# A streaming-encoder block on one core: the second FFN starts with a seven-product pair instead of three token-wise chunks

## The chip, the core and the metric

One NeuronCore of a Trainium2 chip runs the whole kernel. The metric is the device time of one execution in microseconds. The profiler's engine names are kept: PE is TensorE (PEld its weight loads), DVE is VectorE, ACT is ScalarE, POOL is GpSimd, SP is SyncE, whose queue issues most of the DMAs.

## What is computed

A residual block on 256 tokens of width 1024, in float32: a first feed-forward network (FFN), a mixer (a gated linear recurrence beside a causal attention with forgetting, joined by gates), a cross-attention to a memory of 256 rows, and a second FFN. Each part normalises its input, and its output once more ahead of the residual addition. The change touches the second FFN and the stages ahead of it that prepare its weights:

```
h = rmsnorm(x, ffn2_pre_g)
gate, up = split(h @ w_in)          # w_in: 1024 x 5632
x = x + 0.5 * rmsnorm((silu(gate) * up) @ w_down, ffn2_post_g)   # w_down: 2816 x 1024
```

## The kernel before

**Split operands.** TensorE gets every float32 operand as two rounded parts, high and low: ScalarE rounds (`S.copy`), VectorE subtracts (`split`, L155; `load_split` for weights, L129). A product of two operands is three matmuls: high by high, high by low, low by high.

**Tokens and chunks.** The tokens lie in two halves of 128 (`h` 0 and 1), the hidden width in `NFF` = 11 chunks of 256. A *unit* is 128 x 1024 values of a weight, 512 KB. A chunk of `w_in` is four units (gate and up columns of eight blocks of 128 rows, two blocks a unit); a chunk of `w_down` is two. `proj_tok` (L177) multiplies one half of the tokens by one chunk in 24 matmuls of 512 columns; `act_evac` (L414) forms silu(gate) times up, `flush` (L391) and `flush_half` (L405) transpose the result, and `down` (L607) adds its 12 matmuls per half to four accumulators in PSUM.

**Pairs by seven products.** `quad` (L426) takes two chunks and the two token halves as a 2 x 2 by 2 x 2 block product and forms it by a Strassen-Winograd scheme: seven block products of 12 matmuls each instead of eight. It needs four mixed sums of the activations (`mixed`, L289, S1 to S4) and four sums of the weights (T1 to T4). In the second FFN before the change, `QUADS_2` pairs chunks 3-4, 5-6, 7-8 and 9-10. For the first three the weight sums are made earlier: while the mixer and the memory read run, `load_step` (L770) loads weights into one of two `wide` buffers over GpSimd's DMA queue, `at` (L783) makes four additions of 128 x 512 on VectorE at the place that `SUMS_AT` (L56) names, and stores the sums in DRAM, again over GpSimd's queue. There are four steps per pair. `quad` then loads the sums over SyncE's queue (`sum_of`, L446). The last pair makes its sums on the spot.

**The start of the second FFN.** Two chunks are multiplied token-wise, first for half 0, then for half 1 (L617 to L624). Half 1 of the input is not there at the start: the memory read's output projection and its post-norm (`post`, L341, with the reciprocal root `rstd_of`, L220) end with `xs[:, 1]`, and `second` (L1333) transposes it with `to_T` (L319) at the 45th matmul of the FFN (`L_F2` = 44). `to_T` makes four transposes into a PSUM bank and then block by block (`gain_split`, L281) the scaled high part on ScalarE and the low part on VectorE. After the two chunks comes chunk 2, beside which `mixed` rebuilds the whole activation as high plus low (L291 to L294, four blocks of 128 x 256 in each of two additions) and forms S1 to S4; then the first down-projection, and then the pairs.

**What sets the order.** Tile orders the instructions of each engine at compile time, by program order as priority and by a model of when they are ready; it may put a ready instruction of later text ahead of one that is not. `after(n)` pins a group behind the n-th matmul of TensorE, `issue_after` behind a given instruction of the same engine. On the chip each engine then goes strictly in that order.

**Buffers.** Eight pairs of high and low weight buffers of one unit, five `raw` landing buffers, two `wide` ones; in PSUM four banks `acc`, two `mm`, two `tr`.

Of the kernel before, what the change touches and what calls it, by code (L numbers as in the profile page):

```python
# [37 lines left out]
L_F2 = 44  # L38
L_OA = 20
# [14 lines left out]
QUADS_2 = (3, 5, 7, 9)  # L54
# [3 lines left out]
    ("br_a", 1), ("mk", 3), ("mq", 0), ("mq", 1),  # L58
# [20 lines left out]
def block_kernel(ctx: ExitStack, tc: tile.TileContext, wts, head_in, gf_in, x_in, mem_in, memT_in, cols, rows, fbias, masks, out):  # L79
# [209 lines left out]
    def mixed(X, full):  # L289

        if full is None:  # L291
            full = [m4([P, 4, T], n="full") for _ in range(2)]
            for f, xh, xl in zip(full, X.h, X.l):
                V.tensor_tensor(out=f, in0=xh.bitcast(F32), in1=xl.bitcast(F32), op=ALU.add)  # L294
        sums = [m4([P, 2, 4, P], n="sums") for _ in range(2)]
        s1_, s2_, s3_, s4_ = (t[:, i] for t in sums for i in range(2))

        def form(o, x, y, op):
            for q in range(2):
                V.tensor_tensor(out=o[:, 2 * q : 2 * q + 2], in0=x(q), in1=y(q), op=op)  # L300
# [12 lines left out]
        for t in sums:  # L313
            hi, lo = m4([P, 2, 4, P], F32R, "sh"), m4([P, 2, 4, P], F32R, "sl")
            split(hi, lo, t)
            out += [(hi[:, i], lo[:, i]) for i in range(2)]
        return out

    def to_T(X, src, h, g, qs=(0, 1)):  # L319

        for q in qs:
            ps = trp()
            for j in range(4):
                kb = 4 * q + j
                PE.transpose(ps[:, j * P : (j + 1) * P], src(kb), ident)  # L325
# [59 lines left out]
    def ffn(w_in, w_dn, X, full, r2, n_tok, i_row, quads, sums, first_half, second_half=None):  # L385
# [39 lines left out]

        def quad(c, n_down):  # L426
# [6 lines left out]
            def two(src):  # L433
                hi, lo = (p.rearrange("p (i n) -> p i n", i=2) for p in parts_of())
                split(hi, lo, src)
                return [(hi[:, i], lo[:, i]) for i in range(2)]

            B11, B21 = [], []

            if ahead:  # L440
                for i in range(4):
                    hi, lo = load_split(wts[_AT[w_in] + 4 * c + i - 4])
                    B11.append((hi[:, :512], lo[:, :512]))
                    B21.append((hi[:, 512:], lo[:, 512:]))

                def sum_of(k):  # L446
                    W = wp.tile([P, 2, D], F32, tag="wide", name=nm("wide"), bufs=2)
                    for q in range(2):
                        with tc.issue_after(loads[-1]):
                            loads.append(nc.sync.dma_start(W[:, q], sums[c][(0, 3, 2, 1)[k], q]).ins)  # L450
                    return two(W[:, 0].rearrange("p (i n) -> p i n", i=2)) + two(W[:, 1].rearrange("p (i n) -> p i n", i=2))

                def lower():
                    out = []
                    for q in range(2):
                        u = _AT[w_in] + 4 * c + 2 * q
                        raw = wp.tile([P, D], F32, tag="raw", name=nm("raw"), bufs=5).rearrange("p (i n) -> p i n", i=2)
                        loads.append(nc.sync.dma_start(raw, wts[u : u + 2, :, 512:].rearrange("i p n -> p i n")).ins)
                        out += two(raw)
                    return out  # L460

                summed = None
            else:
                wide, made = [], [[], [], []]
# [47 lines left out]

            def block(h, j):
                hs = slice(h * P, h * P + P)
                return lambda i: (X.hi(2 * i + j)[:, hs], X.lo(2 * i + j)[:, hs])

            def F(h, l):
                return lambda i: (h[:, i], l[:, i])

            def prod(ps, A, B, i, start, stop=False):  # L520
                (ah, al), (bh, bl) = A(i), B[i]
                MM(ps, ah, bh, start=start and i == 0, stop=False, skip_group_check=True)
                MM(ps, ah, bl, start=False, stop=False, skip_group_check=True)
                MM(ps, al, bh, start=False, stop=i == 3, skip_group_check=True)

            def prods(ps, A, B, start, stop=False):
                for i in range(4):
                    prod(ps, A, B, i, start, stop)

            def keep(ps):  # L530
                t = sp.tile([P, 512], F32, tag="z2", name=nm("keep"), bufs=3)
                S.copy(t, ps)  # L532
                return t
# [91 lines left out]
        accs = grow = None  # L625
        done = 0
        if callable(r2):
# [6 lines left out]
            n_tok = 2  # L634
        for c in range(n_tok, NFF):
            if c in acts:
                continue
            if c in quads:
                quad(c, done)
                done += 2  # L640
                continue
# [26 lines left out]
            if accs is None:  # L668
                accs = [[acc(), acc()], [acc(), acc()]]
# [80 lines left out]
    def half(X, r, h, g, *ms):  # L750

        for i, m in enumerate(ms):
            with after(m):
                to_T(X, x_blocks(h), h, g, (i,) if len(ms) == 2 else (0, 1))
# [7 lines left out]
    ffn("f1_in", "f1_dn", X1, full1, norm_1, 0, 0, QUADS_1, None, first)  # L762


    sums = {c: dp.tile([4, 2, P, D], F32, name=f"sums_{c}") for c in QUADS_2[:3]}
# [563 lines left out]
    half(X4, r4, 0, G_F2, m + L_MO)  # L1329
# [3 lines left out]
    def second(m):  # L1333
        half(X4, r4, 1, G_F2, m + L_F2)

    ffn("f2_in", "f2_dn", X4, None, r4, 2, 3, QUADS_2, sums, None, second)


# [83 lines left out]
```

## Time and profile before

| | |
|---|---|
| median of 3 runs | 780.89 us (780.45 to 781.83) |
| profiled execution | 780.96 us |
| its span, first to last instruction | 779.2 us |
| granted clock of TensorE | 0.998 |
| TensorE busy | 770.3 us (99%) |
| VectorE busy | 648.4 us (83%) |
| ScalarE busy | 472.4 us (61%) |
| GpSimd busy | 38.7 us (5%) |
| bytes moved by DMA | 182.07 MB, 234 GB/s on average |

A busy time counts the time in which an instruction of the engine is under way; matmuls overlap in the records (each lasts about 0.39 us and the next one issues 0.23 us after it), so TensorE can be 99% busy with some time to spare. The chain that ended last says, from the last instruction backwards, what each step waited for. In the rows of the timeline come start, length, engine, line, operation, output and inputs, and in brackets the idle time of the engine ahead of it with what ended it. A row of busy time by stretches has the stretch, its length, then for each engine busy time and instructions, the granted clock, the share of the DMA engines and GB/s.

### The profile page before, as it was taken

How to read it: one execution, taken by the hardware profiler on the slowest of the kernel's cores; microseconds unless marked ns; L12 is line 12 of the kernel's file. 1: busy time of each engine (PE TensorE's matmuls, PEld its weight loads, DVE VectorE, ACT ScalarE, POOL GpSimd, SP SyncE). 2: the span in 40 equal slices, each digit the busy share in tenths (PEclk: the TensorE clock that was granted, in tenths of full speed). 3: DMA queues.
4: the chain of work that ended last, by engine and by line, in shares of the span. 5: the costliest groups of instructions: out<-in, count | busy, mean ns of one | idle time of the engine just before them, and what ended most of it. 6: DMA issues, size and time to landing. Idle time of an engine off the chain costs nothing.

```text
span 779.2 us, 13049 instructions
## 1 busy us (share of the span) xinstructions
PE 770.3 (99%) x4984; PEld 666.1 (85%) x4984; DVE 648.4 (83%) x995; ACT 472.4 (61%) x711; POOL 38.7 (5%) x64
## 2 busy tenths in 40 slices
PE   9999999999999999999999999999999999999996
PEld 7888878888899999998888888999888888888885
DVE  7799999998886788678787885988767988888994
ACT  7666676577753545447675444744655767777572
POOL 0000000000121000200001220001000000000000
PEclk9999999999999999999999999999999999999999
DMA  9774648378687663754489998468644199779421
GB/s 344 286 264 135 243 143 328 108 231 309 250 289 246 199 211 111 259 189 150 155 309 314 381 337 338 134 223 318 218 154 144 68 341 385 294 283 348 171 81 55
DMA packets 53966, 182.07 MB, mean 234 GB/s; under 512 B 5896, under 2 KB 9360, under 8 KB 53904
## 3 DMA queue, kind: packets, MB, share of 16 engines
q1 hardware_dynamic: 46960, 156.45, 56.6%
q0 software_dynamic: 6800, 24.65, 8.9%
q8 instruction: 39, 0.64, 0.3%
q14 instruction: 23, 0.19, 0.1%
q10 hardware_dynamic: 144, 0.13, 0.0%
HBM read 167.58 MB, written 13.64 MB: 233 GB/s over the span
## 4 chain that ended last, share of the span: by engine, by line
PE 91%; DVE 6%; issue 1%; ACT 1%; DMA 1%; SPq 0%; DVEq 0%; ACTq 0%
PE mm L93 60%; PE acc L93 25%; PE tr L93 3%; DVE lo L157 2%; PE tr L325 1%; PE tr L400 1%; DMA head<-in_head_dram 1%; DVE lo L138 1%; DVE wide L502 1%; ACT hi L156 0%; DVE sum L467 0%; DVE sum L471 0%; DVE sum L489 0%; PE tr L1093 0%; DVE at L421 0%
## 5 line engine op out<-in xcount | busy, mean ns | idle before, releaser
L138 DVE TENSOR_TENSOR lo<-raw,hi 128x1024 fp32r<-128x1024 f32 (+1 forms) x216 | 255.8, 1203 | 49.3 <-ACT hi L137 46.4
L137 ACT CAST hi<-raw 128x1024 fp32r<-128x1024 f32 (+1 forms) x216 | 218.1, 1034 | 94.4 <-PE mm L93 64.5
L93 PE MATMUL mm<-lo,hT 128*128 128x512 f32 (+1 forms) x424 | 161.8, 385 | 0.0
L93 PE MATMUL mm<-hi,hT 128*128 128x512 f32 (+1 forms) x424 | 161.6, 385 | 0.0
L93 PE MATMUL mm<-hi,lT 128*128 128x512 f32 (+1 forms) x424 | 160.5, 383 | 0.0
L93 PE MATMUL acc<-hi,act 128*128 128x512 f32 x352 | 113.2, 390 | 0.0
L93 PE MATMUL mm<-hT,lo 128*128 128x256 f32 x384 | 109.2, 284 | 0.4 <-issue 0.4
L93 PE MATMUL mm<-lT,hi 128*128 128x256 f32 x384 | 109.2, 284 | 0.0
L93 PE MATMUL mm<-hT,hi 128*128 128x256 f32 x384 | 108.9, 283 | 0.0
L93 PEld LDWEIGHTS mm<-hi,hT 128*128 128x128 f32 x424 | 79.6, 188 | 15.3 <-ACT hT L286 0.8
L93 PEld LDWEIGHTS mm<-hi,lT 128*128 128x128 f32 x424 | 79.6, 188 | 15.0 <-DVE lT L287 0.5
L93 PEld LDWEIGHTS mm<-lo,hT 128*128 128x128 f32 x424 | 79.5, 188 | 14.1
L93 PEld LDWEIGHTS acc<-hi,act 128*128 128x128 f32 x352 | 65.9, 188 | 13.5
L93 PEld LDWEIGHTS mm<-hT,lo 128*128 128x128 f32 x384 | 73.6, 192 | 0.6 <-issue 0.6
L93 PEld LDWEIGHTS mm<-lT,hi 128*128 128x128 f32 x384 | 73.6, 192 | 0.2
L93 PEld LDWEIGHTS mm<-hT,hi 128*128 128x128 f32 x384 | 73.6, 192 | 0.1
L93 PE MATMUL acc<-lo,act 128*128 128x512 f32 x176 | 69.1, 393 | 0.0
L156 ACT CAST hi<-wide 128x1024 fp32r<-128x1024 f32 x40 | 41.5, 1054 | 12.8 <-DVE wide L502 9.2
L157 DVE TENSOR_TENSOR lo<-wide,hi 128x1024 fp32r<-128x1024 f32 x40 | 47.7, 1217 | 0.4
L93 PE MATMUL mm<-hi,sh 128*128 128x512 f32 x112 | 43.9, 392 | 0.3 <-ACT keep L532 0.3
L93 PE MATMUL mm<-lo,sh 128*128 128x512 f32 x112 | 43.7, 390 | 0.0
L93 PE MATMUL mm<-hi,sl 128*128 128x512 f32 x112 | 43.6, 389 | 0.0
(249 smaller groups left out, 1146.6 us busy)
## 6 DMA issues: line engine op xcount, KB each, us to landing
raw<-in_wts_dram SPq DMA_DIRECT2D x226, 512.0 KB, 5.1
sums<-wide POOLq DMA_DIRECT2D x24, 512.0 KB, 6.9
wide<-sums SPq DMA_DIRECT2D x24, 512.0 KB, 6.5
wide<-in_wts_dram SPq DMA_DIRECT2D x20, 512.0 KB, 6.6
wide<-in_wts_dram POOLq DMA_DIRECT2D x20, 512.0 KB, 6.7
raw<-in_gf_dram SPq DMA_DIRECT2D x12, 344.0 KB, 5.7
head<-in_head_dram SPq DMA_DIRECT2D x8, 388.0 KB, 6.0
grow<-in_rows_dram SPq DMA_DIRECT2D x4, 512.0 KB, 6.9
```

Of the source, the lines that this page charges most:

```text
L93: log.append(PE.matmul(*args, **kw).ins)
L137: S.copy(h, r)
L138: V.tensor_tensor(out=l, in0=r, in1=h.bitcast(F32), op=ALU.subtract)
L156: S.copy(hi, src)
L157: V.tensor_tensor(out=lo, in0=src, in1=hi.bitcast(F32), op=ALU.subtract)
L325: PE.transpose(ps[:, j * P : (j + 1) * P], src(kb), ident)
L400: PE.transpose(trv[:, j, h * P : (h + 1) * P], ats[c, h][:, j * P : (j + 1) * P], ident)
L502: V.tensor_tensor(out=W[:, :, 0], in0=W[:, :, 0], in1=W[:, :, 1], op=ALU.add)
```

## The change

- The second FFN multiplies only chunk 0 token-wise. `quad_first` takes chunks 1-2 as a pair: its two products of half 0 alone come first, then chunk 0 for half 0, the transposes of half 1 (still at the 45th matmul), chunk 0 for half 1, the product of half 1 alone (T4), the down-projection of chunk 0, and then the four products of mixed sums.
- `QUADS_2` gets chunk 1: five pairs, four of them with sums made ahead. `SUMS_AT` gets four more steps (`br_b` 1, `mk` 1, `mv` 1, `ao` 0), the steps of chunk 1 first in line.
- Of the first pair's four weight sums, T4 and T1 are split into high and low parts on GpSimd (`pool=True`); all other splits stay on ScalarE and VectorE.
- `to_T` can build the whole activation (`full`): four scaled copies on ScalarE into `full`, then one `split` of 128 x 512; for the first four blocks of half 1 it goes block by block as before and adds high and low afterwards. `mixed` no longer rebuilds it.
- The token-wise start for `n_tok` chunks is gone. Helper functions of `quad` move out of it unchanged.

```diff
-QUADS_2 = (3, 5, 7, 9)
+QUADS_2 = (1, 3, 5, 7, 9)
+L_H0 = 4
+L_H1 = 10
 SUMS_AT = (
     ("i_a", 1), ("f_a", 0), ("f_a", 2), ("f_a", 3), ("gates", 1), ("gates", 3), ("br_a", 0), ("br_b", 0),
-    ("br_a", 1), ("mk", 3), ("mq", 0), ("mq", 1),
+    ("br_a", 1), ("br_b", 1), ("mk", 1), ("mk", 3), ("mq", 0), ("mq", 1), ("mv", 1), ("ao", 0),
 )
...
-    def split(hi, lo, src):
-        S.copy(hi, src)
-        V.tensor_tensor(out=lo, in0=src, in1=hi.bitcast(F32), op=ALU.subtract)
+    def split(hi, lo, src, pool=False):
+        (G.tensor_copy if pool else S.copy)(hi, src)
+        (G if pool else V).tensor_tensor(out=lo, in0=src, in1=hi.bitcast(F32), op=ALU.subtract)
...
     def mixed(X, full):
-        if full is None:
-            full = [m4([P, 4, T], n="full") for _ in range(2)]
-            for f, xh, xl in zip(full, X.h, X.l):
-                V.tensor_tensor(out=f, in0=xh.bitcast(F32), in1=xl.bitcast(F32), op=ALU.add)
...
-    def to_T(X, src, h, g, qs=(0, 1)):
+    def to_T(X, src, h, g, qs=(0, 1), full=None):
+        hs = slice(h * P, h * P + P)
         for q in qs:
             ps = trp()
...
+            if full and (h, q) != (1, 0):
+                for j in range(4):
+                    kb = 4 * q + j
+                    S.activation(full[q][:, j, hs], ps[:, j * P : (j + 1) * P], AF.Copy, scale=cols_s[:, g + kb : g + kb + 1])
+                split(X.h[q][:, :, hs], X.l[q][:, :, hs], full[q][:, :, hs])
+                continue
             for j in range(4):
                 gain_split(X, 4 * q + j, ps[:, j * P : (j + 1) * P], g, h * P, h * P + P)
+            if full:
+                V.tensor_tensor(out=full[q][:, :, hs], in0=X.h[q][:, :, hs].bitcast(F32), in1=X.l[q][:, :, hs], op=ALU.add)
...
+        def sum_ahead(c, k, pool=False):
+            W = wp.tile([P, 2, D], F32, tag="wide", name=nm("wide"), bufs=2)
+            for q in range(2):
+                with tc.issue_after(loads[-1]):
+                    loads.append(nc.sync.dma_start(W[:, q], sums[c][(0, 3, 2, 1)[k], q]).ins)
+            return sum((two(W[:, q].rearrange("p (i n) -> p i n", i=2), pool) for q in range(2)), [])
...
+        def quad_first():
+            for k in range(3):
+                acts[k] = m4([P, 2, 2, T], F32R, "act")
+            B11, B21 = left_ahead(1)
+            b1, b3 = mm(), acc()
+            m = len(log)
+            for i in range(4):
+                prod(b1, block(0, 0), B11, i, True)
+                prod(b3, block(0, 1), B21, i, True, True)
+            p1 = keep(b1)
+            V.tensor_tensor(out=p1, in0=p1, in1=b3, op=ALU.add)
+            act_evac(p1, 1, 0)
+            ps = acc()
+            proj_tok(ps, X, chunk(w_in, 0), 0)
+            second_half(m)
+            act_evac(ps, 0, 0)
+            T4 = sum_ahead(1, 3, True)
+            n = len(log)
+            ps = acc()
+            proj_tok(ps, X, chunk(w_in, 0), 1)
+            flush_half(0, 0, n + L_H0)
+            act_evac(ps, 0, 1)
+            late.clear()
+            ready = mixed(X, full)
+            mix.append(ready)
+            (s1h, s1l), (s2h, s2l), (s3h, s3l), (s4h, s4l) = ready
+            T1 = sum_ahead(1, 0, True)
+            n = len(log)
+            b4 = acc()
+            prods(b4, block(1, 1), T4, True, True)
+            u = keep(b4)
+            flush_half(0, 1, n + L_H1)
+            accs[:] = [[acc(), acc()], [acc(), acc()]]
+            for h in range(2):
+                down(0, h)
+            b2 = mm()
+            prods(b2, F(s1h, s1l), T1, True)
+            prods(b1, F(s2h, s2l), sum_ahead(1, 1), False)
+            w = keep(b1)
+            prods(b1, F(s3h, s3l), sum_ahead(1, 2), False, True)
+            v = keep(b1)
+            V.tensor_tensor(out=u, in0=u, in1=v, op=ALU.add)
+            V.tensor_tensor(out=v, in0=b2, in1=v, op=ALU.subtract)
+            act_evac(u, 1, 1)
+            act_evac(v, 2, 1)
+            prods(b2, F(s4h, s4l), lower_ahead(1), False, True)
+            V.tensor_tensor(out=w, in0=b2, in1=w, op=ALU.subtract)
+            act_evac(w, 2, 0)
...
-        for c in range(n_tok):
-            acts[c] = m4([P, 2, 2, T], F32R, "act")
-        for h in range(2):
-            m = len(log)
-            for c in range(n_tok):
-                act_tok(c, h)
-            if h == 0 and n_tok:
-                second_half(m)
...
+        if not first_half:
+            quad_first()
+            done = 1
...
-    sums = {c: dp.tile([4, 2, P, D], F32, name=f"sums_{c}") for c in QUADS_2[:3]}
+    sums = {c: dp.tile([4, 2, P, D], F32, name=f"sums_{c}") for c in QUADS_2[:4]}
...
-    half(X4, r4, 0, G_F2, m + L_MO)
+    full4 = [m4([P, 4, T], n="full") for _ in range(2)]
+    half(X4, r4, 0, G_F2, m + L_MO, full=full4)
...
-    ffn("f2_in", "f2_dn", X4, None, r4, 2, 3, QUADS_2, sums, None, second)
+    ffn("f2_in", "f2_dn", X4, full4, r4, 3, QUADS_2, sums, None, second)
```

More of the change, by code (lines that the diff above doesn't have):

```diff
@@ new lines, in sum_ahead, with lower_ahead @@
+        def sum_ahead(c, k, pool=False):
[4 more added lines that the diff above has]
+            return sum((two(W[:, q].rearrange("p (i n) -> p i n", i=2), pool) for q in range(2)), [])
+        def lower_ahead(c):
+            out = []
+            for q in range(2):
+                u = _AT[w_in] + 4 * c + 2 * q
+                raw = wp.tile([P, D], F32, tag="raw", name=nm("raw"), bufs=5).rearrange("p (i n) -> p i n", i=2)
+                loads.append(nc.sync.dma_start(raw, wts[u : u + 2, :, 512:].rearrange("i p n -> p i n")).ins)
+                out += two(raw)
+            return out
@@ new lines, in prods, with keep @@
+        def prods(ps, A, B, start, stop=False):
+            for i in range(4):
+                prod(ps, A, B, i, start, stop)
+        def keep(ps):
+            t = sp.tile([P, 512], F32, tag="z2", name=nm("keep"), bufs=3)
+            S.copy(t, ps)
+            return t
+        def quad_first():
[4 more added lines that the diff above has]
+            m = len(log)
+            for i in range(4):
+                prod(b1, block(0, 0), B11, i, True)
[39 more added lines that the diff above has]
+            act_evac(w, 2, 0)
@@ L431, in quad @@
                 acts[k] = m4([P, 2, 2, T], F32R, "act")
[L433 to L438, printed above, removed]
             if ahead:
[L441 to L444, printed above, removed]
+                B11, B21 = left_ahead(c)
                 def sum_of(k):
[L447 to L451, printed above, removed]
-                def lower():
[L454 to L460, printed above, removed]
+                    return sum_ahead(c, k)
+                def lower():
+                    return lower_ahead(c)
                 summed = None
             else:
+                B11, B21 = [], []
                 wide, made = [], [[], [], []]
@@ L511, in quad @@
             first = []
[L513 to L533, printed above, removed]
             last = c == NFF - 2
@@ L633, in ffn @@
                     act_evac(outs[c][h], c, h)
-            n_tok = 2
-        for c in range(n_tok, NFF):
+        for c in range(2, NFF):
             if c in acts:
@@ L638, in ffn @@
             if c in quads:
+                if grow is None and sums:
+                    grow = load_row(i_row)
                 quad(c, done)
@@ L667, in ffn @@
                         nc.sync.dma_start(masks_s, masks)
[L668 removed]
+            if not accs:
                 accs = [[acc(), acc()], [acc(), acc()]]
```

35 lines of the change are left out of this document (28 added, 7 removed).

## The prediction

> **What bounds the kernel now.** I read the page first: the span, the busy shares, and the chain that ended last.
>
> ```profile
> span 779.2 us, 13049 instructions
> PE 770.3 (99%) x4984; PEld 666.1 (85%) x4984; DVE 648.4 (83%) x995; ACT 472.4 (61%) x711; POOL 38.7 (5%) x64
> PE 91%; DVE 6%; issue 1%; ACT 1%; DMA 1%; SPq 0%; DVEq 0%; ACTq 0%
> ```
>
> TensorE carries 91% of the chain, so a matmul less counts wherever TensorE is not then kept waiting. Next the chain of waits in order of time, over the start of the second FFN and one later pair.
>
> ```profile
> 597.04 10.44 PE mm L93 x45
> 607.47 0.87 PE tr L325 x8
> 608.35 18.22 PE mm L93 x79
> ...
> 632.03 5.48 PE acc L93 x24
> ...
> 677.08 2.72 PE acc L93 x12
> ```
>
> Twelve 512-column matmuls issue in 2.72 us, 0.2267 us each. From 597.04 to 637.51 only TensorE stands in the chain: matmuls and transposes back to back. So nothing of other engines is waited for at the place that the change rewrites, and whatever it leaves uncovered there is lost at once. Then the table of busy time by stretches: the stage from its first matmul to the first pair, and a steady pair.
>
> ```profile
> core 0: us, PE busy (x) PEld busy (x) DVE busy (x) ACT busy (x) POOL busy (x), PEclk, DMA share, GB/s
> 596.88:637.51 40.63, 40.63 (x186) 32.96 (x185) 37.34 (x77) 26.64 (x46) 0.00 (x0) 1.00 0.51 183
> 674.32:705.25 30.93, 30.93 (x141) 25.48 (x141) 25.63 (x28) 22.62 (x28) 0.00 (x0) 1.00 0.84 318
> ```
>
> The clock is 1.00 throughout. VectorE is busy 37.34 of 40.63 us (92%) at the start and 25.63 of 30.93 us (83%) in a steady pair. GpSimd is idle in both. VectorE is the engine with the least to spare where the work is moved.
>
> **The change part by part.** *The matmuls.* Before, chunks 0, 1 and 2 take 3 x 2 x 24 = 144 matmuls and the first down-projection 24: 168 ahead of the first pair. After, chunk 0 takes 48, the pair 7 x 12 = 84 and the same down-projection 24: 156. Twelve fewer, -2.72 us. That is certain by count; the rest is what stands open.
>
> *The two weight sums on GpSimd.* Each sum is two units of 128x1024, each a one-input copy and a two-input subtraction: eight GpSimd instructions. Their data come early, and their buffers are the ones that the first products release, unit by unit from 596.88 + 6 x 0.2267, about 598.3 us. The last are due at TensorE's 73rd matmul (first sum, about 614 us) and 109th (second, about 623 us), so their own length is covered. Behind them wait the loads of the pair's next two sums, which take over the two `wide` buffers, and in SyncE's queue behind those the weights of chunk 3.
>
> ```profile
> wide<-sums SPq DMA_DIRECT2D x24, 512.0 KB, 6.5
> ```
>
> If GpSimd ends near 613 to 617, these land by 624 (6.5 us); the third product wants the later one near 631. That holds. What GpSimd does to VectorE is not covered. GpSimd's nearest instructions of this size are two selects at 327.53, and I looked at VectorE beside them.
>
> ```profile
> 327.53 3.88 POOL L1053 TENSOR_SCALAR_AFFINE_SELECT cbm<-cbm 128x1024 f32<-128x1024 f32 x2 [6.58 <-DMA cbm<-cd]
> ```
>
> ```profile
> 327.21 1.22 DVE L138 TENSOR_TENSOR lo<-raw,hi 128x1024 fp32r<-128x1024 f32 x1
> ...
> 328.55 1.90 DVE L138 TENSOR_TENSOR lo<-raw,hi 128x1024 fp32r<-128x1024 f32 x1
> 330.38 0.14 DVE L225 TENSOR_SCALAR y<-v 128x1 int32<-128x1 int32 x1
> 330.55 0.86 DVE L227 SCALAR_TENSOR_TENSOR t<-v,y 128x1 f32<-128x1 f32 x1
> 331.45 0.16 DVE L229 SCALAR_TENSOR_TENSOR y<-t,y 128x1 f32<-128x1 f32 x1
> 331.65 0.22 DVE L231 SCALAR_TENSOR_TENSOR t<-v,y 128x1 f32<-128x1 f32 x1
> ```
>
> The split at 328.55 takes 1.90 us where the one before it took 1.22, and a 128x1 operation takes 0.86 where its like takes 0.22; both have two inputs in SBUF. The one-input 128x1 operation at 330.38 stays at 0.14. So I read it as turns: the first select holds VectorE off from 328.43 (327.21 + 1.22) to 329.23 (328.55 + 0.68), 0.80 us, and the second from 330.45 to 331.19, 0.74 us. By the Trainium skill (SBUF — State Buffer, "Who interferes with whom") a VectorE instruction with two SBUF inputs and a GpSimd instruction that reads SBUF shut each other out for a whole instruction. The trace agrees, by 1.90 against 1.22 us.
>
> I take 0.8 us of hold for a copy and twice that, 1.6, for a subtraction, which reads two inputs (an estimate from these rows): 4 x 0.8 + 4 x 1.6 = 9.6 us. The lower bound is 0 if everything falls into VectorE's gaps, the upper 8 x 1.96 (3.88 / 2, waiting included) = 15.7. In exchange VectorE is rid of four splits of 1.2 us, but against the old start it gains as many others (below).
>
> The Trainium skill (GPSIMD Engine Reference, section 3.1) gives 4497 ns for a two-input addition of 2048 elements; half of that, an estimate of 2.25 us each, would add 4 x 0.65 = 2.6 us of hold and, by the share used below, 1.95 us to the sum. No run here shows that operation yet.
>
> Now what VectorE does from 598.85 on, in its timeline and in the table of stretches:
>
> ```profile
> 599.43 0.68 DVE L348 SCALAR_TENSOR_TENSOR post<-acc,grow 128x512 f32<-128x512 f32 x1
> 600.02 0.21 DVE L227 SCALAR_TENSOR_TENSOR t<-v,y 128x1 f32<-128x1 f32 x1
> 600.30 0.61 DVE L287 SCALAR_TENSOR_TENSOR lT<-tr,cols_s,hT 128x128 fp32r<-128x128 f32 x2
> ...
> 601.88 1.21 DVE L138 TENSOR_TENSOR lo<-raw,hi 128x1024 fp32r<-128x1024 f32 x1
> ...
> 604.98 1.42 DVE L352 SCALAR_TENSOR_TENSOR xs<-post,y,xs 128x512 f32<-128x512 f32 x2
> ```
>
> ```profile
> 598.85:606.39 7.54, 7.54 (x34) 6.15 (x33) 7.16 (x26) 4.36 (x10) 0.00 (x0) 1.00 0.56 199
> ```
>
> This is the tail of the memory read's post-norm: two reciprocal-root chains, each with five tiny operations of two inputs (L227 to L235), and then the second half of `xs`, ready at 606.39 us. The transposes of that half start at 607.47, 44 matmuls into the FFN, in TensorE's own order: everything behind them waits with them, and there is no other matmul for half 1. The slack is 1.1 us. The change leaves these chains where they are, saves here five `lT` operations (1.5 us) and adds one of 0.65: without GpSimd `xs` would come at 605.5. About 2.0 us of this stretch (two L348 and the one-input operations) can run beside GpSimd. If the first sum (4.8 us) and half of the second (2.4) get their turns before `xs`, VectorE loses 7.2 - 2.0 = 5.2 us: `xs` at 610.7, TensorE **3.3 us** late at 607.47. Were all eight ahead of it, 9.6 - 2.0 gives 613.1 and 5.6 us; were they all hidden, 0. I take the middle: turns favour GpSimd, since a tiny operation uses one up, but the second sum's buffers come free last.
>
> *The transposed gain of half 0.* Its first four blocks now become four scaled copies, one 128x512 rounding and one subtraction, before any matmul; the old way hands over block by block.
>
> ```profile
> 594.94 0.37 ACT L286 ACTIVATE hT<-tr,cols_s 128x128 fp32r<-128x128 f32 x1
> ...
> 597.85 0.64 ACT L286 ACTIVATE hT<-tr,cols_s 128x128 fp32r<-128x128 f32 x2
> ```
>
> ```profile
> 596.88 0.39 PE L93 MATMUL mm<-hi,hT 128*128 128x512 f32 x1
> ```
>
> Run without a break from 594.94, four copies at 0.3 us, a rounding and a subtraction (0.55 and 0.65 us each as queued) end at 597.3, when the third matmul wants them: 0. With ScalarE's present order, where the fourth block starts at 597.85, they end near 599.3: 2.0 us late. The transposes behind it start that much later too, so this and the wait for `xs` are not added: the larger one, 3.3, stands for both.
>
> *Two copies of a bank with nothing to cover them.* In a steady pair the down-projection runs while ScalarE copies bank `b1`; the new start has used it up, and the third product writes `b1` again at once; the fourth, into `b2`, needs that bank read by VectorE.
>
> ```profile
> 682.13 0.39 PE L93 MATMUL mm<-hi,sl 128*128 128x512 f32 x1
> 682.36 0.39 PE L93 MATMUL acc<-hi,act 128*128 128x512 f32 x1
> ```
>
> ```profile
> 682.55 0.59 ACT L532 COPY keep<-mm 128x512 f32<-128x512 f32 x1 [0.26 <-PE mm L93]
> ...
> 687.99 0.59 ACT L532 COPY keep<-mm 128x512 f32<-128x512 f32 x1 [0.26 <-PE mm L93]
> ```
>
> ```profile
> 688.91 0.68 DVE L565 TENSOR_TENSOR keep<-mm,keep 128x512 f32<-128x512 f32 x1
> ```
>
> There the second product's last matmul issues at 682.13, and the next matmul, of the down-projection, at 682.36. Without it the next would wait for the end of the copy at 683.14: 0.8 us for `w`. For `v` the copy's 0.8 and two VectorE operations of 0.65 follow, 2.1 us; Tile may put the next pair's first products there, so I take half, 1.0. Bounds for the two: 0 (all filled) and 2.9.
>
> *Four more steps of sums in the middle.* Each is four additions on VectorE, four DMAs of 512 KB on GpSimd's queue and no matmul.
>
> ```profile
> 448.93 0.68 DVE L792 TENSOR_TENSOR wide<-wide 128x512 f32<-128x512 f32 x1
> ...
> 451.58 0.68 DVE L795 TENSOR_TENSOR wide<-wide 128x512 f32<-128x512 f32 x1
> ```
>
> ```profile
> 449.00:480.00 31.00, 31.00 (x146) 25.63 (x145) 23.60 (x29) 13.65 (x15) 6.28 (x10) 1.00 0.95 351
> 497.10:519.00 21.90, 21.90 (x185) 21.90 (x185) 20.34 (x50) 16.18 (x32) 0.00 (x0) 1.00 0.47 148
> 560.00:575.00 15.00, 14.91 (x93) 13.03 (x92) 11.12 (x14) 10.70 (x21) 0.00 (x0) 1.00 0.31 106
> 575.00:591.00 16.00, 16.00 (x74) 13.29 (x74) 6.66 (x9) 5.72 (x10) 0.00 (x0) 1.00 0.39 132
> ```
>
> Four at 0.65, about 2.7 us. The steps at `br_b` 1, `mv` 1 and `ao` fall into stretches with 7.4, 3.9 and 9.3 us of VectorE free. `mk` 1 falls into 497 to 519 with 1.6 free: up to 1.1 us, taken as 0.5. The DMA share of 0.95 at 449 could make the `br_b` step wait for its load; the weights behind it have the emptier stretch after 480, so 0.
>
> *The rest* is hidden: `full` built by ScalarE takes two additions off VectorE, the banks turn over as before, and the pairs from chunk 3 on are unchanged.
>
> **The sum.** -2.72 + 3.3 + 0.8 + 1.0 + 0.5 = +2.9 us. The profiled execution took 780.96 us (span 779.2 and 1.8 around it), 0.07 over the median of 780.89; so 780.89 + 2.9 = **783.8 us**.
>
> **The rivals.**
> *Faster.* GpSimd's instructions find VectorE's gaps. For it: 37.34 of 40.63 still leaves 3.3 us, and the saving in `lT` widens it. The place is `xs` of half 1; it decides at 1.1 us of slack plus 0.9 saved, 2.0 us of loss. With that wait at 0, `v` filled by the next pair, and `mk` free: -2.72 + 0.8 = 779.0, at best 778.2. Against it: two-input operations are most of VectorE's list there.
> *About even.* The hold is small but the two copies are paid in full: -2.72 + 2.1 + 0.5, 780.8, reaching from 779.4 to 782.4.
> *Slower elsewhere.* VectorE as a whole becomes the bound. From 596.88 on it needs 37.34 + two more splits (2.4) + four combinations (2.4) - `full` and `lT` (4.0) = 38.1 us in a stage of 40.63 - 2.72 = 37.9, plus about 6.6 of hold that is not beside other work. The lead in splits (six at 1.2, 7.2 us) can swallow 6.8; if half of that is lost, 3.4 us go at the first full pair: -2.72 + 3.4 + 1.8 + 0.5 = 783.9, with 783 to 787 around it, and `xs` on time.
>
> **How the numbers follow.** Forecast (a late `xs`) 0.52, with a range of its own of 782.5 to 789.5 (the upper bound for the hold, 15.7, with some of it covered); faster 0.22; even 0.14; slower elsewhere 0.12. Under 0.2% (1.6 us) a measurement of this kernel can't tell from no change. Faster 0.22, same 0.14, slower 0.64. To leave out no more than 2 in 10 the range must reach into the faster case: 778.4 to 789.5.
>
> **What would show it.** In the new profile: TensorE waiting ahead of the second half's transposes (about 3 us, released by `xs` on VectorE); splits and 128x1 operations on VectorE longer than 1.22 and 0.22 while GpSimd works; waits of 0.8 to 2 us on `keep` at the third and fourth products. The forecast is wrong if VectorE's durations stay as they are beside GpSimd, if `xs` is there at 607.5, or if the next pair's products fill both waits.

## The result: 790.08 us, 1.2% slower, and the profile after

The changed kernel takes 790.08 us (median of 5 runs, 788.7 to 790.57) against 780.45 us (779.81 to 781.83) for the kernel before on the same chip: a ratio of 1.0119, 95% interval 1.0104 to 1.0133. The forecast was 783.8, slower. The direction holds; the time lies 0.6 us above the range.

First the page of the kernel after: span, busy time and the chain that ended last.

```profile
span 788.5 us, 13113 instructions
PE 771.4 (98%) x4972; PEld 666.6 (85%) x4972; DVE 670.3 (85%) x1008; ACT 478.6 (61%) x721; POOL 65.0 (8%) x88
PE 86%; DVE 8%; issue 2%; ACT 1%; DMA 1%; DVEq 0%; ACTq 0%; SPq 0%
```

TensorE's instructions went from 4984 to 4972, the twelve counted; its share of the chain fell from 91% to 86%, and VectorE's rose from 6% to 8%. To find the place, I measure one stage in every kernel: from the last sixteen matmuls of the stage before (`tr` x16 in the chain) to the first row of twelve matmuls of the pair of chunks 5-6 (`mm` x12, the steady pair of the prediction's table). Before:

```profile
573.66 1.92 PE tr L93 x16
...
674.32 2.76 PE mm L93 x12
```

and after:

```profile
574.18 1.92 PE tr L95 x16
...
683.52 2.76 PE mm L95 x12
```

That is 100.66 us before and 109.34 after, 8.7 us of a span that is 9.3 longer. Everything that matters is in this stage. In the timeline of TensorE after, the rows with a wait (in brackets) are these:

```profile
597.77 0.50 PE L95 MATMUL mm<-hi,hT 128*128 128x512 f32 x1 [0.25 <-ACT hT L158]
602.58 0.50 PE L95 MATMUL mm<-hi,lT 128*128 128x512 f32 x1 [0.86 <-DVE lT L159]
609.24 0.50 PE L95 MATMUL acc<-lo,hT 128*128 128x512 f32 x1 [0.25 <-DVE lo L140]
616.72 1.97 PE L324 MATMUL tr<-ident,xs 128*128 128x128 f32 x8 [6.74 <-DVE xs L359]
```

TensorE stands still for 6.74 us ahead of the transposes of half 1, released by `xs` on VectorE: the wait that was forecast, at twice its length. What holds `xs` up stands in the timelines of GpSimd and of VectorE.

```profile
599.58 1.04 POOL L158 CAST hi<-wide 128x1024 fp32r<-128x1024 f32 x1 [15.32 <-PE acc L95]
600.94 1.04 POOL L158 CAST hi<-wide 128x1024 fp32r<-128x1024 f32 x1 [0.32 <-issue]
601.95 6.16 POOL L159 TENSOR_TENSOR lo<-wide,hi 128x1024 fp32r<-128x1024 f32 x2
608.05 3.02 POOL L158 CAST hi<-wide 128x1024 fp32r<-128x1024 f32 x2
611.03 4.63 POOL L159 TENSOR_TENSOR lo<-wide,hi 128x1024 fp32r<-128x1024 f32 x2
```

```profile
599.62 1.01 DVE L237 SCALAR_TENSOR_TENSOR y<-t,y 128x1 f32<-128x1 f32 x1
...
601.33 1.19 DVE L159 TENSOR_TENSOR lT<-full,hT 128x512 fp32r<-128x512 f32 x1
...
602.57 3.29 DVE L140 TENSOR_TENSOR lo<-raw,hi 128x1024 fp32r<-128x1024 f32 x1
605.78 0.14 DVE L227 TENSOR_SCALAR y<-v 128x1 int32<-128x1 int32 x1
605.84 3.35 DVE L140 TENSOR_TENSOR lo<-raw,hi 128x1024 fp32r<-128x1024 f32 x1
609.11 0.99 DVE L229 SCALAR_TENSOR_TENSOR t<-v,y 128x1 f32<-128x1 f32 x1
...
610.62 0.46 DVE L231 SCALAR_TENSOR_TENSOR y<-t,y 128x1 f32<-128x1 f32 x1
611.11 2.27 DVE L233 SCALAR_TENSOR_TENSOR t<-v,y 128x1 f32<-128x1 f32 x1
613.42 2.26 DVE L235 SCALAR_TENSOR_TENSOR t<-t 128x1 f32<-128x1 f32 x1
615.72 0.16 DVE L237 SCALAR_TENSOR_TENSOR y<-t,y 128x1 f32<-128x1 f32 x1
615.91 1.41 DVE L359 SCALAR_TENSOR_TENSOR xs<-post,y,xs 128x512 f32<-128x512 f32 x2
```

The two lists read as turns: all eight GpSimd instructions lie ahead of `xs`, and eight VectorE operations with two inputs are long. Against their usual lengths (0.16 and 0.22 for 128x1, 0.69 for 128x512, 1.2 for a split) they lost 0.85, 0.5, 2.1, 2.15, 0.77, 0.3, 2.05 and 2.1 us, 10.8 together. The two of 128x1 at 611.11 and 613.42 are the plainest: nothing but waiting out one GpSimd subtraction each. The one-input operation at 605.78 keeps its 0.14 us, and an operation of 128x512 with one of its two inputs in PSUM (`keep<-keep,acc` at 610.02) its 0.68.

After the wait TensorE is slow for a while. In the table of stretches the column behind the five engines is the granted clock:

```profile
609.86:616.72 6.86, 0.12 (x2) 0.00 (x1) 6.72 (x8) 0.51 (x1) 5.80 (x4) 0.82 0.64 233
616.72:622.36 5.64, 5.64 (x22) 4.80 (x22) 4.15 (x15) 4.76 (x14) 0.00 (x0) 0.62 0.49 181
622.36:640.00 17.64, 17.64 (x81) 14.21 (x79) 17.26 (x25) 14.08 (x18) 0.00 (x0) 1.00 0.30 105
```

The clock is 0.62 over the 5.64 us behind the wait and 1.00 after that; matmuls start 0.43 us apart (619.34, 619.76, 620.19 in the timeline) where 0.2267 is usual. The Trainium skill (TensorE: Matmul & The Clock Gate, Part 1) has the clock fall to half after an idle window of about 3.4 us; 6.74 us of idling and the 0.43 agree; in e7 and e10, below, the same clock follows much shorter waits.

So the stage adds up: -2.72 for the twelve matmuls, +1.8 for the three small waits (the spacing of the matmuls around them, 0.64 + 1.25 + 0.63, less 3 x 0.2267), +6.9 for `xs` (7.14 less 0.23), about +2.3 for the half clock; 8.3 of 8.7 us.

### The profile page after: what moved, and what is told of

It is laid out like the page before. It is cut to its first block, busy times and chain, and to the rows that moved or that the text cites. A ratio compares the mean times of both kernels' runs of the same rounds, so it can differ in the third digit from the quotient of the medians.

```text
span 788.5 us, 13113 instructions
## 1 busy us (share of the span) xinstructions
PE 771.4 (98%) x4972; PEld 666.6 (85%) x4972; DVE 670.3 (85%) x1008; ACT 478.6 (61%) x721; POOL 65.0 (8%) x88
## 4 chain that ended last, share of the span: by engine, by line
PE 86%; DVE 8%; issue 2%; ACT 1%; DMA 1%; DVEq 0%; ACTq 0%; SPq 0%
PE mm L95 56%; PE acc L95 25%; PE tr L95 3%; DVE lo L159 2%; DVE lo L140 2%; DMA raw<-in_wts_dram 1%; PE tr L324 1%; PE tr L407 1%; DVE wide L591 1%; ACT hi L158 1%; DVE sum L556 0%; DVE sum L560 0%; DVE sum L578 0%; PE tr L1157 0%; DVE at L428 0%
## 5 line engine op out<-in xcount | busy, mean ns | idle before, releaser
L95 PE MATMUL mm<-hi,lT 128*128 128x512 f32 (+1 forms) x380 | 143.8, 383 | 0.9 <-DVE lT L159 0.9
L95 PE MATMUL mm<-hi,hT 128*128 128x512 f32 (+1 forms) x380 | 144.4, 383 | 0.3 <-ACT hT L158 0.2
L95 PE MATMUL mm<-lo,hT 128*128 128x512 f32 (+1 forms) x380 | 144.4, 384 | 0.0
L95 PEld LDWEIGHTS mm<-hi,lT 128*128 128x128 f32 x380 | 71.3, 188 | 14.2 <-DVE lT L159 1.3
L95 PEld LDWEIGHTS mm<-hi,hT 128*128 128x128 f32 x380 | 71.4, 188 | 13.9 <-ACT hT L158 0.7
L95 PEld LDWEIGHTS mm<-lo,hT 128*128 128x128 f32 x380 | 71.2, 188 | 12.4
L159 DVE TENSOR_TENSOR lo<-wide,hi 128x1024 fp32r<-128x1024 f32 x44 | 52.4, 1220 | 0.5
L861 POOL DMA_DIRECT2D sums<-wide x32 | 23.6, 738 | 347.1 <-DVE wide L858 236.7
L95 PE MATMUL mm<-hi,sh 128*128 128x512 f32 x128 | 50.3, 393 | 0.1
L95 PE MATMUL mm<-lo,sh 128*128 128x512 f32 x128 | 50.1, 391 | 0.0
```

The costliest lines, as they stand in the source:

```text
L95: log.append(PE.matmul(*args, **kw).ins)
L159: (G if pool else V).tensor_tensor(out=lo, in0=src, in1=hi.bitcast(F32), op=ALU.subtract)
L861: G.dma_start(sums[u][2 * e : 2 * e + 2, q, :, i * 512 : i * 512 + 512].rearrange("k p n -> p k n"), W[:, e])
```

## The experiments

The theory (*the lock*): GpSimd's eight instructions shut VectorE's two-input operations out, and `xs` is late by that. The rivals: *amount* (VectorE and ScalarE have too little time for the new start, whoever does the splits), and, once the clock was seen, *the clock* (the slow matmuls behind the wait are a cost of their own). A second question came up on the way: where the gain of twelve matmuls goes once the lock is gone. All ratios are to the kernel before, measured beside each kernel (4 to 12 runs of each), with 95% intervals. The stage is the one measured above, from one profiled execution of each; the same code ahead of it begins the stage between 572.80 and 574.45 us, so spans compare less well than stages.

| kernel | median us | ratio | stage us |
|---|---|---|---|
| before (medians of its batches) | 780.45 to 780.99 | 1 | 100.66 |
| after | 790.08 | 1.0119 (1.0104 to 1.0133) | 109.34 |
| e1_no_pool | 781.02 | 1.0002 (0.9992 to 1.0011) | 100.75 |
| e2_pool_copies | 784.18 | 1.0041 (1.0026 to 1.0056) | 104.29 |
| e3_before_idle_pool | 790.53 | 1.0119 (1.0104 to 1.0134) | 109.50 |
| e4_pool_after_xs | 789.37 | 1.0107 (1.0092 to 1.0122) | 109.90 |
| e5_pool_held | 787.16 | 1.0078 (1.0061 to 1.0094) | 106.28 |
| e6_dve_after_xs | 780.99 | 1.0002 (0.9993 to 1.0011) | 100.69 |
| e7_dve_after_xs_blocks | 783.29 | 1.0026 (1.0017 to 1.0036) | 103.07 |
| e8_warm | 790.19 | 1.0117 (1.0102 to 1.0132) | 109.60 |
| e9_no_splits | 780.86 | 1.0000 (0.9991 to 1.0009) | 100.19 |
| e10_copies_held | 786.01 | 1.0061 (1.0048 to 1.0073) | 105.40 |
| e11_no_splits_xs | 780.23 | 0.9995 (0.9986 to 1.0004) | 99.31 |
| e12_act_after_hT | 781.22 | 1.0005 (0.9996 to 1.0014) | 100.05 |

### Without GpSimd (e1), and with half of it (e2)

```diff
-            T4 = sum_ahead(1, 3, True)
+            T4 = sum_ahead(1, 3)
...
-            T1 = sum_ahead(1, 0, True)
+            T1 = sum_ahead(1, 0)
```

> The changed kernel with its two GpSimd splits back on ScalarE and VectorE, all else as changed. Theory L (lock): what delays the second half of xs is GpSimd's reading of SBUF, which shuts out VectorE's two-input operations; without it no VectorE split is longer than 1.25 us and no 128x1 operation longer than 0.25 us. Tile puts three of the four splits (3 x 1.2 us) ahead of xs, so xs comes near 609 to 611 instead of 616.7, TensorE waits 1 to 3 us for it, and the time falls to 781 to 785 us. Theory A (amount): VectorE simply has too much to do there, GpSimd relieves it; then the four splits make xs later still and the time is over 790 us.

```diff
-        (G if pool else V).tensor_tensor(out=lo, in0=src, in1=hi.bitcast(F32), op=ALU.subtract)
+        V.tensor_tensor(out=lo, in0=src, in1=hi.bitcast(F32), op=ALU.subtract)
```

> The changed kernel with only the four rounding copies on GpSimd, the four subtractions on VectorE. Theory L: a copy holds VectorE off for about 0.8 us, a subtraction for about 2.05 us (2.27 less 0.22 in the changed kernel), so 8.2 us of hold go and 3.6 us of VectorE work ahead of xs come: xs about 3 to 5 us earlier than in the changed kernel, 784 to 787 us, between the changed kernel and the one without GpSimd. Theory A: later than the changed kernel, over 790 us.

The rows of TensorE at the transposes of half 1, first of e1, then of e2:

```profile
609.71 1.31 PE L324 MATMUL tr<-ident,xs 128*128 128x128 f32 x8 [0.46 <-DVE xs L359]
```

```profile
610.74 1.32 PE L324 MATMUL tr<-ident,xs 128*128 128x128 f32 x8 [1.96 <-DVE xs L359]
```

With the same work on ScalarE and VectorE the wait is 0.46 us and the time that of before (781.02, within the lock's 781 to 785): *amount* does not explain the 9 us. Four copies on GpSimd cost 3.5 us of stage over e1 (0.9 each), the whole change 8.6; 784.18 is within the lock's range too.

### The kernel before, with eight GpSimd instructions that nobody needs (e3)

```diff
+    idle = [mp.tile([P, D], F32, tag="m4", name=f"idle_{i}") for i in range(2)]
+    G.memset(idle[0], 0.0)
+    G.tensor_copy(idle[0][:, 0:1], X4.lo(4, 0, 1).bitcast(F32))
+    for _ in range(4):
+        G.tensor_copy(idle[1], idle[0])
+        G.tensor_tensor(out=idle[1], in0=idle[0], in1=idle[1], op=ALU.subtract)
```

> The kernel before, unchanged in its computation, with eight GpSimd instructions of the same kinds and sizes (four copies, four subtractions of 128x1024) on two scratch tiles, which nothing reads; they start when the fifth block of half 0 is transposed. Theory L: xs of half 1 comes 6 to 10 us late, TensorE waits 5 to 9 us ahead of the second half's transposes, and the time rises to 786 to 791 us although nothing that is computed waits for GpSimd. Theory A: nothing changes, 780 to 781 us.

VectorE, GpSimd and TensorE of e3:

```profile
604.40 2.35 DVE L233 SCALAR_TENSOR_TENSOR t<-t 128x1 f32<-128x1 f32 x1
...
608.10 2.19 DVE L231 SCALAR_TENSOR_TENSOR t<-v,y 128x1 f32<-128x1 f32 x1
```

```profile
599.83 2.40 POOL L1335 TENSOR_TENSOR idle<-idle,idle 128x1024 f32<-128x1024 f32 x1
...
607.93 2.34 POOL L1335 TENSOR_TENSOR idle<-idle,idle 128x1024 f32<-128x1024 f32 x1
```

```profile
614.40 1.97 PE L325 MATMUL tr<-ident,xs 128*128 128x128 f32 x8 [7.28 <-DVE xs L352]
```

This settles the cause. The instructions feed nothing and wait for nothing that anyone else needs, and they alone make the kernel before as slow as the change does, by the same wait at the same place. The ratio is 1.0119 in both, though the change has twelve matmuls less: what it saves by them it loses elsewhere, as e1 shows.

### GpSimd's splits behind `xs` (e4, e5)

The edit of e5, at T4:

```diff
+            hold = G.tensor_copy(sp.tile([P, 1], F32, tag="s1", name="hold", bufs=16), xs[:, 1, D - 1 : D]).ins
+            with tc.issue_after(hold):
-            T4 = sum_ahead(1, 3, True)
+                T4 = sum_ahead(1, 3, True)
```

> The changed kernel, with one more GpSimd copy of 128x1 from the finished second half of xs ahead of the splits in GpSimd's queue, so that they begin only after xs. Theory L: xs is there at 606 to 608 and the wait of 6.7 us ahead of the transposes is gone; the same hold (about 11 us) now falls on the mixed sums and the first product that needs GpSimd's own output (due about 614 us), so part of it comes back as waits there: 781 to 787 us. Theory A: xs as late as in the changed kernel, 790 us.

e4 had the copy in the text but no `issue_after`. Tile put it behind the splits, and everything stayed as after: it tells nothing of the theory. e5 has the edge as shown, for T1 too.

> The changed kernel with GpSimd's splits held behind the second half of xs, this time with an ordering edge on GpSimd's queue: in the kernel before this one Tile had put the copy from xs behind the splits, so that nothing was delayed. Theory L (lock): the wait of 6.7 us ahead of the transposes shrinks to under 1 us, xs comes at 605 to 608; the hold of about 11 us now meets the splits of the second half, the mixed sums and the weights, and TensorE waits there, or for GpSimd's own output (first sum due about 614 us): 782 to 788 us. Theory D (delay is not the lock but the amount of work ahead of xs): xs and the time stay as in the changed kernel, 790 us.

TensorE's row of e5 with the largest wait, and two rows of VectorE:

```profile
613.72 0.80 PE L95 MATMUL acc<-hi,lT 128*128 128x512 f32 x1 [4.72 <-DVE lT L289]
```

```profile
607.82 2.31 DVE L231 SCALAR_TENSOR_TENSOR y<-t,y 128x1 f32<-128x1 f32 x1
610.16 2.26 DVE L233 SCALAR_TENSOR_TENSOR t<-v,y 128x1 f32<-128x1 f32 x1
```

`xs` is on time and its wait gone, but the next reciprocal-root chain meets the same lock, and `lT` of half 1 stands in VectorE's order among it. The wait moved behind the transposes, to the first matmuls of half 1, and cost 5.6 us of stage over e6.

### TensorE kept busy through the wait (e8)

```diff
+            keep_warm = acc()
+            with after(m + L_F2):
+                for _ in range(30):
+                    warm_last = PE.matmul(keep_warm[:, :P], ones, ones, start=True, stop=True).ins
+            with tc.issue_after(warm_last):
-            second_half(m)
+                second_half(m)
```

> The changed kernel with 30 matmuls of 128x128 ones into a spare accumulator bank ahead of the second half's transposes, whose output nothing reads. They fill the wait for xs, they don't shorten it. Theory K (clock): after the idle 6.7 us the granted clock is 0.62 for 5.6 us, the transposes take 1.97 us instead of 0.87 and eleven matmuls 3.67 instead of 2.49; kept busy, TensorE goes on at full clock and the time falls by about 2.3 us, to 787 to 788.5 us. Rival W: these matmuls are slow because their operands come late; then nothing changes, 790 us, and the added matmuls can only cost.

```profile
610.02 6.86 PE L502 MATMUL acc<-ones 128*128 128x128 f32 x60
616.95 1.32 PE L324 MATMUL tr<-ident,xs 128*128 128x128 f32 x8
...
620.50 0.49 PE L95 MATMUL acc<-hi,lT 128*128 128x512 f32 x1 [1.00 <-DVE lT L289]
```

The transposes take 1.32 us in place of 1.97 and the granted clock is 1.00 over 610 to 625, so here the idling does cause the half clock. The 30 matmuls make 60 records. The time does not fall (790.19, where 787 to 788.5 was expected; stage 109.60 against 109.34): a TensorE at full speed comes too early for `lT` of half 1 and waits 1.00 us there. In the change the half clock lay beside the hand-over of half 1 and was no loss of its own.

### Where the gain of twelve matmuls went (e6, e7, e9 to e12)

e6 is the change without GpSimd, and with VectorE's splits of T4 and T1 pinned behind the last operation of `xs`:

```diff
-            T4 = sum_ahead(1, 3, True)
+            with tc.issue_after(xs_last[0]):
+                T4 = sum_ahead(1, 3)
```

> The changed kernel without GpSimd's splits, and the four splits of these sums held on VectorE's queue behind the second half of xs. Theory L says that what is left to lose in the kernel without GpSimd is these splits standing ahead of xs: xs at 605 to 607 instead of 610.3, no wait for it, and 2.72 us of matmuls less at last show: 777.8 to 779.8 us. Rival S (start-up): the start gives the gain back in other waits whatever the order, because VectorE and ScalarE are full from 596 to 620: 780 to 782 us.

`xs` is there in time; TensorE's pauses in e6 are 0.25 us at the start, and these two:

```profile
612.75 0.50 PE L96 MATMUL acc<-hi,hT 128*128 128x512 f32 x1 [0.61 <-ACT hT L289]
...
630.58 0.50 PE L96 MATMUL mm<-hi,sh 128*128 128x512 f32 x1 [0.45 <-ACT keep L482]
```

Without these pauses and the slower restart behind each the stage would be 100.66 - 2.72 = 97.9 us; it is 100.7, and the time, 780.99, lies in the start-up rival's range. ScalarE now ends the waits. e7 is e6 with half 0 handed over block by block:

```diff
-            if full and (h, q) != (1, 0):
+            if full and (h, q) == (1, 1):
```

> The kernel just described, and half 0 of the input handed over block by block again (only the last four blocks of half 1 go through the whole activation). If the copies into the whole activation delay the first products, as the prediction's bound of 2.0 us has it, the waits for hT and lT at 597 to 603 (1.1 us in the changed kernel) go and it is 0.5 to 1 us below the other; the whole activation then costs three more additions of 0.6 us on VectorE, which can eat this: from -1 to +1 us against the other.

The start's wait is gone, but three others come at half 1, and it is slower by 2.4 us of stage, outside the -1 to +1 that was expected.

```profile
611.99 0.50 PE L96 MATMUL acc<-hi,hT 128*128 128x512 f32 x1 [0.93 <-ACT hT L289]
613.11 0.50 PE L96 MATMUL acc<-hi,lT 128*128 128x512 f32 x1 [0.38 <-DVE lT L290]
614.14 0.80 PE L96 MATMUL acc<-hi,hT 128*128 128x512 f32 x1 [0.53 <-ACT hT L289]
```

Behind them the granted clock is 0.54 from 614.14 to 617.38 and matmuls start 0.43 us apart: about 1.5 of the 2.4 us, though no run shows what the stage would be without that. Why the handing over of half 0 makes half 1 later was not followed up.

e9 leaves the loads and splits of T4 and T1 out, to see whether the gain then shows:

```diff
-            T4 = sum_ahead(1, 3, True)
+            T4 = [blk(chunk(w_in, 0), i) for i in range(4)]
...
-            T1 = sum_ahead(1, 0, True)
+            T1 = T4
```

> Leaves out the loads and the splits of T4 and T1 of the first pair: both products take the first four blocks of chunk 0's weights, already split, in their place (so the pair's values are other ones). Every matmul stays, nothing runs on GpSimd. Question: where does the gain of twelve matmuls (2.72 us) go, when e1 and e6 take as long as the kernel before? Theory S (the start has too little of ScalarE and VectorE for the two more splits): with eight instructions of 1.0 to 1.2 us less there, the waits of e1 and e6 between 596 and 615 shrink and the time falls to 777.5 to 779.5 us (ratio 0.996 to 0.999). Rival H (the hand-over of half 1 itself, from the transposes by the scaled copies, the rounding and the subtraction of whole 128x512 blocks, costs the gain whatever else is in the queues): 780 to 781.5, with the same pauses around the transposes.

It does not: Tile moved three of the next splits up into the chain of `xs` (at 604.70, 605.97 and 607.65 in VectorE's timeline), which came at 610.2 us, so e9 is no clean test. e11 pins the splits of the down-projection and of T2 behind `xs` as well:

```diff
+            with tc.issue_after(xs_last[0]):
+                chunk_dn = [unit(w_dn, i) for i in range(2)]
+                T2 = sum_ahead(1, 1)
```

> Like e9, the loads and splits of T4 and T1 are left out (both products take the first four blocks of chunk 0's weights, so the values are other ones), and now VectorE's next four splits (two of the down-projection's weights, two of T2) are pinned behind the end of xs, as in e6. In e9 those four moved up into the chain of xs and xs came at 610.2 all the same. Theory S (the two engines have too little for the two more splits): with xs on time and eight instructions less, 778 to 779.5 us. Rival H (the hand-over of half 1 by whole 128x512 blocks takes the gain whatever else is queued): 780 to 781.5, with TensorE's pauses of e6 between 607 and 613.

Its stage is 99.31 us: half of the 2.72 us is there, and half is lost at the start (`hT` of half 0) and in short pauses, most of them at half 1. The time, 0.9995 (0.9986 to 1.0004), is not told from no change, and its 780.23 us lies in rival H's range. Read from one stage each, the two more splits take about half of the gain (100.7 in e6, 99.3 here) and the hand-over the rest; the times do not show it.

e10 gives ScalarE's four copies to GpSimd behind `xs` and leaves the subtractions on VectorE; e12 keeps them on ScalarE and puts those of T1 and of the down-projection behind the hand-over of half 1:

```diff
+            hold = G.tensor_copy(sp.tile([P, 1], F32, tag="s1", name="hold", bufs=16), xs[:, 1, D - 1 : D]).ins
+            with tc.issue_after(hold), tc.issue_after(xs_last[0]):
+                T4 = sum_ahead(1, 3, True)
```

> e6 with the four rounding copies of T4 and T1 on GpSimd, behind the end of xs, and the subtractions on VectorE, behind the end of xs. A trial for a kernel that beats the one before: ScalarE is 12.9 of 13.0 us busy in e6 where half 1 is handed over. If ScalarE is what is short there (theory A): 779 to 780 us, the wait for hT at the first matmuls of half 1 gone. If GpSimd's copies take from VectorE what they give ScalarE (theory L, 0.8 us of hold a copy on two-input operations, as in e2): 781.5 to 784, with the wait at lT of half 1 instead.

```diff
+            with tc.issue_after(xs_last[0]), tc.issue_after(hT_last[-1]):
+                T1 = sum_ahead(1, 0)
+                for i in range(2):
+                    unit(w_dn, i)
```

> e6 (no splits on GpSimd, VectorE's splits of T4 and T1 behind the end of xs) with ScalarE's casts of T1 and of the down-projection's two weight units pinned behind the last operation that builds half 1. All of the change's work stays. If the casts of 1 us between the blocks of half 1 make the pauses of e6 at 609 to 613 (about 1.3 us): 779 to 780.3 us, and a version that is faster than before by 0.1 to 0.2%. If the pauses are the length of the hand-over itself, or the casts are late for the products that need them (620 to 631): 780.5 to 782.5.

With four copies on GpSimd e10 is 4.7 us of stage slower than e6, 786.01 us where at most 784 was expected. VectorE's rows show three operations of 128x1 at a copy's length each.

```profile
608.22 1.03 DVE L230 SCALAR_TENSOR_TENSOR t<-v,y 128x1 f32<-128x1 f32 x1
609.29 0.95 DVE L232 SCALAR_TENSOR_TENSOR y<-t,y 128x1 f32<-128x1 f32 x1
610.28 0.95 DVE L234 SCALAR_TENSOR_TENSOR t<-v,y 128x1 f32<-128x1 f32 x1
```

But the wait for `lT` of half 1 that follows from them is only 1.29 us. TensorE's two other waits come when GpSimd has long ended (at 611.2):

```profile
623.26 0.50 PE L96 MATMUL mm<-hi,sh 128*128 128x512 f32 x1 [1.39 <-ACT hi L159]
624.71 0.80 PE L96 MATMUL mm<-lo,sh 128*128 128x512 f32 x1 [0.95 <-DVE lo L160]
```

Thirteen matmuls of mixed sums stand ahead of the last twenty of the down-projection here, where in e6 all stand behind it, and their weight splits are late; the granted clock is 0.50 from 624.71 to 627.98. So the 4.7 us are not the price of four copies alone, and how this order came about was not followed up.

e12 gains 0.6 us of stage over e6 and nothing that its time shows: 781.22 us, in the range for pauses that the hand-over's own length makes. No version tried is faster than the kernel before by more than the measurement can tell.

## Why the prediction was right in direction and short in size

- *The matmuls, -2.72:* counted rightly, but a gain only on paper. Where nothing holds `xs` up (e1, e6) the stage is as long as before. The prediction charged 0.8 and 1.0 for later steps and 0 for the start's hand-over except as part of the `xs` wait; the runs put the loss at the start, in the hand-over and, as far as e11's stage tells, the two more splits.
- *The late `xs`, +3.3: the step that failed, by its size.* The mechanism, its place and its releaser were as forecast (after, e3). But counted from the start of the stage, the transposes of half 1 came 42.54 us in, where they had come 33.81 in: 8.7 us late, not 3.3. The hold before `xs` was taken as 7.2 us less 2.0 beside other work, 5.2; the rows add up to 10.8. Three parts of it were wrong. A subtraction holds VectorE 2.05 to 2.15 us, not 1.6: the four took 8.4 us, not 6.4, and the four copies 2.4, not 3.2. The Trainium skill's figure (GPSIMD Engine Reference, section 3.1), 2.25 us for one by the estimate in the prediction, was the nearer: e3's subtractions take 2.34 to 2.40 us where VectorE does not stretch them. All eight instructions came before `xs`, not three quarters (2.4 us); the rows read as if the chain that `xs` ends, slowed by its own waits, so stays beside GpSimd. And hardly any of it was free, where 2.0 us had been expected to be, since tiny two-input operations waited out GpSimd's instructions, some of them nearly whole.
- *The half clock:* not forecast. After a wait of 6.7 us it is in the trace, about 2.3 us, but by e8 it is no loss of its own here.
- *The hand-over of half 0:* said to be covered by the larger wait. It cost 0.25 us at `hT` and, with GpSimd beside it, 0.86 at `lT`, both ahead of the wait for `xs`. These are part of the 8.7 us: without them TensorE would have come earlier and waited longer for the same `xs`. That is an argument; no run takes them out and leaves `xs` late.
- *`w` and `v`, +0.8 and +1.0:* neither shows as a wait in the change. In its timeline of TensorE, matmuls of the next pair's first products and transposes stand between the second product of mixed sums and the third, and more of the next pair's between the third and the fourth. The prediction had named this as a sign of being wrong.

```profile
639.95 0.39 PE L95 MATMUL mm<-hi,sl 128*128 128x512 f32 x1
640.18 0.39 PE L95 MATMUL tr<-hi,hT 128*128 128x512 f32 x1
...
641.02 0.50 PE L95 MATMUL mm<-hi,sh 128*128 128x512 f32 x1
...
643.69 0.39 PE L95 MATMUL mm<-hi,sl 128*128 128x512 f32 x1
643.91 0.39 PE L95 MATMUL tr<-hi,lT 128*128 128x512 f32 x1
...
647.99 0.39 PE L95 MATMUL mm<-hi,lT 128*128 128x512 f32 x1
648.22 0.39 PE L95 MATMUL mm<-hi,sh 128*128 128x512 f32 x1
```

- *The four more steps of sums, +0.5:* not seen. The stage begins at 574.18 us after and 573.66 before, and the kernels with the same four steps scatter from 572.80 to 574.45. So 2.3 us of the forecast, with `w` and `v`, do not show in the stage; without them it would have been 781.5. That it came within 6.3 us of the result is in part luck: terms that were too high made up for one that was far too low.
- *The rivals:* faster, even and slower elsewhere are out as forecasts for this kernel. But the even case's time, 780.8, is what the change gives without GpSimd (781.0 in e1 and e6), by another mechanism: the two copies were to take 2.1 us of the gain, and the only wait for one that is marked, at the third product of e6, is 0.45 us. Two figures in the prediction are off and decide nothing: paid in full, `w` and `v` are 2.9 by its own bound, where the even case adds 2.1; and 3.88 / 2 is 1.94, so the upper bound for the hold is 15.5.

## What to carry to other kernels

An idle engine is not free help when its instructions hold up the engine that ends the critical chain. In this kernel a GpSimd instruction that reads SBUF had to be priced at nearly its full length on VectorE's two-input operations, however small these were (2.27 us for one of 0.22): look where it falls, not how much it does. To test such a price, put the suspected instructions into the kernel before with scratch data: e3 gave the answer in one run. And a count of matmuls removed is an upper bound; what is gained is what the hand-overs around them let through.

## What the runs showed of the hardware that was not expected

- A chain of dependent two-input 128x1 operations beside GpSimd goes at one operation per GpSimd instruction: 2.27 and 2.26 us (after), 2.31 and 2.26 (e5), 1.03, 0.95 and 0.95 beside copies (e10), against 0.15 to 0.22.
- A GpSimd copy of 128x1024 takes 1.04 us and a subtraction 2.34 to 2.40 us when VectorE lets them run; VectorE stretches them in turn (a subtraction of 3.32 us in e3).
- The granted clock falls behind waits far shorter than the change's 6.74 us: in e7 to 0.54 for 3.2 us behind waits of 0.93, 0.38 and 0.53 us, in e10 to 0.50 for 3.3 us behind 1.39 and 0.95 us.
- Thirty small matmuls on spare operands hold the granted clock at 1.00 over 6.9 us of waiting (e8).
